# Output projection of an adaLN block as Strassen block products, with all later conditioning sums moved beside the convolution

## The chip, the cores and the metric

The kernel runs as one program on one core of a Trainium2 chip. The metric is the device time of one execution in microseconds (us). TensorE (PE) multiplies, VectorE (DVE) and ScalarE (ACT) work on tiles in on-chip memory, GpSimd (POOL) here mostly issues DMAs that add to what they land on ("accumulate"), and SyncE (SP) issues the plain DMAs. Each engine carries out its instructions in program order; a semaphore wait holds everything behind it on that engine. PEld is the loading of weights into the PE array, which overlaps the matmuls.

## What is computed

One block with 512 tokens and width 2048, all in fp32:

```python
sh_a, sc_a, g_a, sh_f, sc_f, g_f = jnp.split(jax.nn.silu(c) @ ada_w[l] + ada_b[l], 6, axis=-1)
h = modulate(rms_norm(x, norm_mix[l]), sh_a, sc_a)
proj = h @ w_in[l]
...
y_conv = short_conv_mixer(cb, cc, ch, conv_w[l])          # u = cc * ch, 3-tap causal conv, times cb
y_conv = rms_norm(y_conv in groups of 128, out_norm_conv)
y_attn = nsa_mixer(q, k..., v..., gates, ...)             # 8 heads of 128, then rms_norm per head
x = x + g_a[:, None, :] * (jnp.concatenate([y_conv, y_attn], axis=-1) @ w_out[l])
h = modulate(rms_norm(x, norm_ffn[l]), sh_f, sc_f)
x = x + g_f[:, None, :] * ((jax.nn.silu(h @ ffn_w1[l]) * (h @ ffn_w3[l])) @ ffn_w2[l])
```

The six conditioning vectors are 2048 wide each. `w_out` is 2048 x 2048, `ffn_w1` and `ffn_w3` are 2048 x 5632, `ffn_w2` is 5632 x 2048.

## The kernel before

**Products.** An fp32 product is made of three matmuls: both factors are split into a high part that PE takes as it is (`hi`, an ACT cast) and the rest (`lo`, a DVE subtraction), and `mm3` (L96 to L100) adds lo x hi, hi x lo and hi x hi into one bank. A weight tile is 128 x 1024 (`load_split`, L86 to L94): one DMA, one cast, one subtraction.

**Conditioning sums.** A product of silu(c) with a 2048-row, 512-column piece of `ada_w` is not made on PE. It is a chain of 16 DVE operations of 128 x 512 (`ada_steps`, L183 and L185), each of which adds one loaded tile times a column of `cT` into `acc`. The 128 partitions are summed afterwards: four PE transposes (L200) and a DVE reduction (L202) where the result is wanted as a column, or a matmul with ones (`ada_bcast`, L252) where it is wanted as a row. The sums for sh_a and sc_a stand at the start of the kernel. Later come 4 sums for g_a and 8 for sh_f and sc_f; the 4 for g_f run during the up projection, by ACT and POOL (`gate_steps`, L209).

**Stages, with their times in the trace.**

- 0 to 195 us: first sums, norm of x, first columns of `w_in`.
- 195 to 306 us: two `token_blocks` (L612; 16 steps of a weight tile), with the preparation of keys and the compressed blocks woven in.
- 306 to 719 us: `convs` (L807): eight `conv(c)` (L760) of eight steps each, one weight tile 128 x 768 per step, with `attention_steps` woven in. Behind each conv's matmuls stands its tail: product, three taps, gate (L783 to L788), square on ACT (L791), a matmul with ones (L793), rsqrt (L123, L124) and the final multiply (L797). Six of the sums for sh_f and sc_f stand one behind each of conv 0 to 5, the first g_a sum behind conv 7.
- 719 to 915 us: the output projection, `token_block(w_out, ...)` for four column blocks n of 512, 32 weight tiles, 768 matmuls of 128 x 512 into four banks `main`, one for each tile of 128 tokens. After each n: `t = ps * ga` (L868), `x = x + t` (L869), the square with its row sum (L870), a store to the spill `xd` (L871), and for n < 3 the transposes of x into `x2T` (L846, L847). The other three g_a sums and the last two of sh_f and sc_f run here.
- 915 to 928 us: the row norms (L881 to L883), a matmul with ones that spreads them over the partitions (`rb`, L884), the last transposes, then `modulated` (L957 on DVE, L958 on ACT) and the splits of the blocks of the normed input (`h_parts`, L948 and L949) that the up projection multiplies.
- 928 to 1799 us: up projection, Strassen's seven block products for eight in 42 of 44 units (`product`, L932 and L934).
- 1799 to 2241 us: down projection, Strassen's scheme over the token halves, column halves and row pairs: 154 steps of 12 matmuls (L1264), in four groups of 6, 6, 5 and 5 row pairs. Its weight sums are made in place by accumulate DMAs on POOL (L1222), its input sums by DVE (L1230 to L1235).

**What sets the order.** The code is unrolled, and each engine gets its instructions in the order in which the Python code issues them; `weave` mixes two generators by a fixed ratio, and `issue_after` puts an instruction behind another of its engine. There is no planner.

Of the kernel before, what the change touches and what calls it, by code (L numbers as in the profile page):

```python
# [17 lines left out]
P = 128  # L18
# [20 lines left out]
CGL = IN_W - P  # L39

# [29 lines left out]
def block_kernel(ctx: ExitStack, tc: tile.TileContext, a: dict, out: bass.AP):  # L70
# [13 lines left out]

    def load_split(ring, src, ko, n):
# [5 lines left out]
        nc.sync.dma_start(raw[:, :m].rearrange("p (k n) -> p k n", k=ko), src)  # L91
        nc.scalar.copy(hi[:, :m], raw[:, :m])  # L92
        nc.vector.tensor_sub(lo[:, :m], raw[:, :m], hi[:, :m].bitcast(F32))  # L93
        return tuple(t[:, :m].rearrange("p (k n) -> p k n", k=ko) for t in (hi, lo))  # L94
# [32 lines left out]
    accp = pool("acc", 2)  # L127
    act_ = ExitStack()
    act = pool("act", KC, stack=act_)

# [7 lines left out]
    for i in range(NT):  # L138
        xt = sp.tile([P, D], F32, name=f"xt{i}")
        nc.sync.dma_start(xt, x[i * P:(i + 1) * P, :])  # L140
        xts.append(xt)
# [19 lines left out]
    shf = cp.tile([P, 2, KC], F32, name="shf")  # L161
    gfc = cp.tile([P, KC], F32, name="gfc")
# [4 lines left out]
    def ada_steps(ring, width, c0, n, bias=False):  # L167


        acc = accp.tile([P, 512], F32, tag="acc", name="acc")[:, :n]  # L170
# [38 lines left out]
    def gate_steps(ring, lag):  # L209

        for n in range(4):
            acc = accp.tile([P, 512], F32, tag="acc", name="acc")
            c0 = 5 * D + n * 512
            for k in range(KC):
                w = ring.tile([P, 512], F32, tag="araw", name="araw") if k else acc
# [3 lines left out]
                yield  # L219
# [4 lines left out]
                for _ in range(lag - 2):  # L224
                    yield
            gate_cols(acc, n)

    def gate_cols(acc, n):

        ps = main()  # L230
# [3 lines left out]
        d = gfc[:, 4 * n:4 * n + 4]  # L234
        b = bcol[:, 5 * KC + 4 * n:5 * KC + 4 * n + 4]
        v = ps.rearrange("p (c q) -> p c q", c=4)
        if n < 2:
# [6 lines left out]
    latest = {}  # L244

    def note(what):
        latest[what] = nc.cur_bb.bb.instructions[-1]

    def ada_bcast(psum_tile, dst, acc):

        ps = psum_tile()
        nc.tensor.matmul(ps, ones, acc, start=True, stop=True)  # L252
        nc.scalar.copy(dst, ps)
# [6 lines left out]
    kvp = ExitStack()  # L260
    kp = pool("kvraw", 1, stack=kvp, side="right")
    ksv = kp.tile([P, NT, 512], F32, name="ksv")
    q0 = kp.tile([P, NT, 512], F32, name="q0")
# [623 lines left out]
    act_.close()  # L887

# [458 lines left out]
```

## Time and profile before

| | |
|---|---|
| median of 3 runs | 2244.02 us (2242.67 to 2246.96) |
| profiled execution: its time, its span | 2242.84 us, 2241.1 us |
| PE busy, DVE busy, ACT busy, POOL busy (share of the span) | 97%, 78%, 48%, 10% |
| mean granted PE clock | 0.989 |
| DMA, mean over the span | 182 GB/s |

The profiler's span leaves out 1.7 us of the execution's own time. A row of the costliest groups reads: line, engine, operation, output <- inputs, shape, how often | busy time in us, mean ns of one | idle time of the engine just ahead of them and what ended it. A timeline row reads: start, length, engine, line, operation, how many in a row, and in brackets the idle time before and what ended it. Matmuls are pipelined and their ends modelled, so PE's pace is read from the distance of their starts. A row of the windows reads: from:to, length, then the busy time and instruction count of PE, PEld, DVE, ACT and POOL, the granted PE clock, the share of the DMA engines and GB/s.

### The profile page before, as it was taken

The numbers are of one execution on the slowest core, as the hardware profiler recorded it, in microseconds if no ns is written. First come the engines' busy times: TensorE is split into PE (matmuls) and PEld (weight loads), VectorE is DVE, ScalarE is ACT, GpSimd is POOL, SyncE is SP. The second block draws the span as 40 slices with busy tenths as digits, with TensorE's granted clock in tenths as the row PEclk, the third lists the DMA queues.
The fourth block names the chain that finished last, engine by engine and source line by source line (L and its number), as shares of the span: only waits on it lengthen the run. The fifth ranks groups of instructions, "written<-read, shape, count | busy, mean of one in ns | idle before, by whom it ended". The sixth has DMA issues, their size and how long they took to land.

```text
span 2241.1 us, 30371 instructions
## 1 busy us (share of the span) xinstructions
PE 2163.3 (97%) x10999; PEld 1811.5 (81%) x10999; DVE 1745.1 (78%) x2677; ACT 1078.4 (48%) x1790; POOL 226.0 (10%) x265
## 2 busy tenths in 40 slices
PE   5899999999999999899999999999999989999998
PEld 5677778778787778788888888888888868888887
DVE  5886857767866773788888888888888866878787
ACT  6544434555444222645555555555554445545453
POOL 2330000000000000000110110110110021111132
PEclk9999999999999999999999999999999999999999
DMA  8985556345544884266665665666665299998888
GB/s 293 295 270 147 163 180 176 111 116 152 154 134 134 272 310 141 75 188 169 164 179 155 174 169 154 171 170 164 165 174 150 75 278 242 214 229 215 227 167 183
DMA packets 386658, 408.95 MB, mean 182 GB/s; under 512 B 18404, under 2 KB 292168, under 8 KB 385484
## 3 DMA queue, kind: packets, MB, share of 16 engines
q1 hardware_dynamic: 358796, 325.22, 47.2%
q0 software_dynamic: 27712, 81.80, 18.7%
q8 instruction: 86, 1.41, 0.3%
q14 instruction: 64, 0.52, 0.1%
HBM read 371.30 MB, written 19.92 MB: 175 GB/s over the span
## 4 chain that ended last, share of the span: by engine, by line
PE 60%; DMA 3%; DVE 1%; ACT 0%; issue 0%; DVEq 0%; SPq 0%; ACTq 0%
PE main L932 14%; PE aux L932 11%; PE aux L1264 9%; PE main L1264 9%; PE main L934 7%; PE aux L934 6%; PE main L98 1%; PE main L99 1%; PE main L100 1%; DMA g<-gd 1%; DMA araw<-in_ada_w 1%; DMA t<-in_ffn_w 1%; DVE acc L185 0%; DMA raw<-in_ffn_w 0%; DMA acc<-in_ada_b 0%
## 5 line engine op out<-in xcount | busy, mean ns | idle before, releaser
L932 PE MATMUL main<-hC,whi 128*128 128x512 f32 x1408 | 355.5, 394 | 3.5 <-DVE hC L949 3.4
L925 DVE TENSOR_TENSOR wlo<-raw,whi 128x1024 fp32r<-128x1024 f32 x218 | 265.7, 1219 | 106.6 <-ACT whi L919 105.2
L919 ACT CAST whi<-raw 128x1024 fp32r<-128x1024 f32 x218 | 228.6, 1049 | 238.4 <-PE main L932 117.6
L932 PEld LDWEIGHTS main<-hC,whi 128*128 128x128 f32 x1408 | 254.0, 190 | 49.9 <-DVE hC L949 4.3
L932 PE MATMUL aux<-hC,whi 128*128 128x512 f32 x1072 | 270.0, 394 | 0.2 <-ACT whi L919 0.2
L932 PEld LDWEIGHTS aux<-hC,whi 128*128 128x128 f32 x1072 | 193.7, 190 | 35.2 <-ACT whi L919 0.4
L98 PE MATMUL main<-alo,whi 128*128 128x512 f32 x448 | 183.3, 410 | 21.3 <-DVE alo L357 21.0
L934 PEld LDWEIGHTS main<-hC,wlo 128*128 128x128 f32 x1408 | 192.1, 190 | 13.7
L934 PE MATMUL main<-hC,wlo 128*128 128x256 f32 x1408 | 196.3, 282 | 0.0
L185 DVE SCALAR_TENSOR_TENSOR acc<-araw,cT,acc 128x512 f32<-128x512 f32 x184 | 137.7, 749 | 71.0 <-DMA araw<-in_ada_w 67.3
L99 PE MATMUL main<-ahi,wlo 128*128 128x512 f32 x448 | 178.3, 398 | 0.0
L100 PE MATMUL main<-ahi,whi 128*128 128x512 f32 x448 | 177.7, 397 | 0.0
L92 ACT CAST whi<-raw 128x1024 fp32r<-128x1024 f32 (+1 forms) x80 | 78.9, 988 | 191.5 <-PE main L100 123.7
L98 PE MATMUL main<-wlo,ahi 128*128 128x512 f32 x384 | 153.2, 399 | 7.3 <-DVE t L868 7.0
L934 PEld LDWEIGHTS aux<-hC,wlo 128*128 128x128 f32 x1072 | 146.4, 190 | 10.5
L100 PE MATMUL main<-whi,ahi 128*128 128x512 f32 x384 | 151.6, 395 | 0.0
L99 PE MATMUL main<-whi,alo 128*128 128x512 f32 x384 | 151.5, 395 | 0.0
L934 PE MATMUL aux<-hC,wlo 128*128 128x256 f32 x1072 | 149.8, 283 | 0.0
L919 ACT CAST whi<-t 128x1024 fp32r<-128x1024 f32 x84 | 88.3, 1051 | 126.8 <-PE aux L932 63.4
L1216 ACT CAST whi<-t 128x1024 fp32r<-128x1024 f32 x88 | 92.6, 1054 | 111.2 <-PE aux L1264 55.0
L93 DVE TENSOR_TENSOR wlo<-raw,whi 128x1024 fp32r<-128x1024 f32 (+1 forms) x80 | 92.0, 1154 | 67.3 <-ACT whi L92 66.7
L1217 DVE TENSOR_TENSOR wlo<-t,whi 128x1024 fp32r<-128x1024 f32 x88 | 107.4, 1221 | 24.6 <-ACT whi L1216 23.9
(307 smaller groups left out, 4390.5 us busy)
## 6 DMA issues: line engine op xcount, KB each, us to landing
raw<-in_ffn_w SPq DMA_DIRECT2D x220, 512.0 KB, 4.3
araw<-in_ada_w SPq DMA_DIRECT2D x300, 256.0 KB, 3.5
t<-in_ffn_w POOLq DMA_DIRECT2D x66, 512.0 KB, 6.0
raw<-in_w_in SPq DMA_DIRECT2D x128, 192.0 KB, 2.8
raw<-in_w_in SPq DMA_DIRECT2D x40, 512.0 KB, 6.3
araw<-in_ada_w SPq DMA_DIRECT2D x40, 512.0 KB, 5.8
raw<-in_w_out SPq DMA_DIRECT2D x32, 512.0 KB, 3.6
acc<-araw POOLq DMA_DIRECT2D x60, 256.0 KB, 4.2
```

What stands on the lines that cost most here:

```text
L93: nc.vector.tensor_sub(lo[:, :m], raw[:, :m], hi[:, :m].bitcast(F32))
L98: nc.tensor.matmul(ps, lhs[0], rhs[1], start=first, stop=False)
L99: nc.tensor.matmul(ps, lhs[1], rhs[0], start=False, stop=False)
L100: nc.tensor.matmul(ps, lhs[0], rhs[0], start=False, stop=last)
L185: nc.vector.scalar_tensor_tensor(acc, w, s, acc, op0=ALU.mult, op1=ALU.add)
L919: nc.scalar.copy(hi, t)
L925: nc.vector.tensor_sub(lo, t, hi.bitcast(F32))
L932: nc.tensor.matmul(ps, wt[0][:, ks[k]], hC[p][:, k, :], start=first and k == 0, stop=False, skip_group_check=True)
L934: nc.tensor.matmul(ps[:, HS:], wt[1][:, ks[k]], hC[p][:, k, 0:HS], start=False, stop=last and k == HK - 1, skip_group_check=True)
L1216: nc.scalar.copy(hi, w)
L1217: nc.vector.tensor_sub(lo, w, hi.bitcast(F32))
L1264: nc.tensor.matmul(ps, a_[l][:, tok], w[r][:, cs], start=begins and m == 0, stop=ends_ and m == 2, skip_group_check=True)
```

## The change

1. **Output projection by block products.** The four token tiles and 2048 columns are halved, and the 16 row blocks of `w_out` are paired (k with k + 8) in two groups of four pairs. `products()`, which the down projection now uses too, makes seven products p for each group, each of four steps k of 12 matmuls (L965): 56 steps, 672 matmuls. For each step `w_split` casts and subtracts the 128 x 1024 weight tile (L919, L921), `a_split` makes the 128 x 256 input sum and its split (L935 to L947), and POOL adds the next weight block onto the tile in memory (L927). Banks are read by `o_read` into `y2` (L1082 to L1091).
2. **Gate and residual.** The g_a sums are turned to columns `gac` and spread to rows by `gate_rows` (L285: 16 DVE diagonals, 16 matmuls with ones of 128 columns). A finished tile of `y2` is multiplied by `ga` (L1099), and POOL adds x to it from memory (L1100). Then follow its square (L1036, ACT) and its store (L1037, POOL).
3. **Turning by diagonal norms.** `row_norms` makes for each token tile a diagonal matrix of its norms (L1048). 64 matmuls of `y2` with it (L1065) transpose and scale at once; ACT applies gain and shift on the way out (L1069, 128 x 256 each). The upper token half goes first, and three half products of the up projection (L1187, L1189) stand ahead of the lower half. `rb` and L957 are gone.
4. **All 12 later sums earlier.** `sums_stream` puts two DVE sum operations (L241, L243) behind each of the 16 token-block steps and two or three behind each of the 64 conv steps: 32 + 160. Their loads are single tiles, staged in buffers not yet in use.
5. **Conv tails.** The square, ones matmul and norm of conv c (L839 to L844) move behind the first steps of conv c + 1; those of conv 7 stand in the output projection's first group.
6. **Buffers.** Four 128 x 2048 tiles `xy` hold in turn x, the raw keys, the conv and attention outputs, the blocks of the normed input, weight pairs of the up projection and T pairs of the down projection.

```diff
+    def sums_stream():
+        jobs = [(lambda acc, n=n: gate_cols(acc, n, 0, gac), 2 * D + n * 512) for n in range(4)]
...
+                w = spare[0]()
+                with tc.issue_after(latest["load"]):
+                    nc.sync.dma_start(w, ada_v[:, k, c0:c0 + 512])
+                with tc.issue_after(latest["lo"]):
+                    if k:
+                        nc.vector.scalar_tensor_tensor(acc, w, cT[:, k:k + 1], acc, op0=ALU.mult, op1=ALU.add)
...
     def convs():
+            for k in range(KC // 2):
+                next(steps_)
+                if k in (0, 2):
+                    next(last, None)
+                for _ in range(2 + k % 2):
+                    next(stream, None)
+                yield
+            last = steps_
...
+    def x2_store(i, n):
+        y = y2[:, i, n * 512:(n + 1) * 512]
...
+        with tc.issue_after(latest["o_hi"]):
+            nc.scalar.activation(sq, y, AF.Square, accum_out=ss2[:, i, n:n + 1])
+        nc.gpsimd.dma_start(xd[n][:, i, :], y)
...
+    def scaled():
+        i, n = scales.pop(0)
+        cs = slice(n * 512, (n + 1) * 512)
+        nc.vector.tensor_mul(y2[:, i, cs], y2[:, i, cs], ga[:, cs])
+        nc.gpsimd.dma_start(y2[:, i, cs], x[i * P:(i + 1) * P, cs], accum_op=ALU.add)
+        turns.append((i, n))
...
+        if b and p == 4:
+            if k == 0:
+                row_norms(0)
+            scaled()
+            x2_store(*turns.pop(0))
+            if k > 1:
+                modulated(0, 0, 4 * k - 8, aux)
+                split_half(0, 0, 4 * k - 8)
...
-        for i, ps in enumerate(pst):
-            nc.vector.tensor_mul(t, ps, ga)
-            nc.vector.tensor_add(x2, x2, t)
-            nc.scalar.activation(t, x2, AF.Square, accum_out=ss2[:, i, n:n + 1])
-        nc.gpsimd.dma_start(xd[n], x2s[n])
...
+    products(w_out, o_groups, ((1, 5, 6, 3, 7, 2, 4), (1, 5, 6, 3, 2, 7, 4)), 1,
...
+    for c in (0, 4):
+        modulated(0, 1, c, aux)
+        split_half(0, 1, c)
...
+    while turns:
+        x2_store(*turns.pop(0))
+    row_norms(1)
...
+    for s in order[:3]:
+        s["mm"](s, (0,))
+    for j in range(2):
+        for c in (0, 4):
+            modulated(1, j, c, (aux, main)[c // 4])
+            split_half(1, j, c)
```

**DVE in the convolution, before:** the weight splits (`wlo`, L772) among attention (L714 to L740) and the sums (L185, `acc <- araw`) that wait their turn behind a conv.

```order
L772 TENSOR_TENSOR wlo<-raw,whi 128x768
L715 TENSOR_REDUCE nm<-aux 128x1
L781 MEMSET u 128x2
L185 SCALAR_TENSOR_TENSOR acc<-araw,cT,acc 128x512
L772 TENSOR_TENSOR wlo<-raw,whi 128x768
L720 RECIPROCAL sm<-sm 128x2
L185 SCALAR_TENSOR_TENSOR acc<-araw,cT,acc 128x512
L721 TENSOR_TENSOR sm<-sm,gts 128x2
```

The same engine in the convolution after the change, where `xy` is the staging buffer and L820 the split:

```order
L241 SCALAR_TENSOR_TENSOR acc_3568<-xy,cT,acc_3568 128x512
L761 TENSOR_REDUCE nm<-aux 128x1
L241 SCALAR_TENSOR_TENSOR acc_3568<-xy,cT,acc_3568 128x512
L820 TENSOR_TENSOR wlo<-raw,whi 128x768
L766 RECIPROCAL sm<-sm 128x2
L241 SCALAR_TENSOR_TENSOR acc_3568<-xy,cT,acc_3568 128x512
L767 TENSOR_TENSOR sm<-sm,gts 128x2
L786 SCALAR_TENSOR_TENSOR o_3438<-aux,sm,o_3438 128x128
L243 TENSOR_SCALAR acc_3944<-xy,cT 128x512
```

The sums now stand in every step between two splits, in all eight convs.

**ACT from the output projection to the up projection, before** (`whi` of L919 is a weight of the up projection, L958 the shift, L948 a split of the normed input):

```order
L870 ACTIVATE t,ss_6478<-x_7214 128x512 x2
L919 CAST whi<-raw 128x1024
L870 ACTIVATE t,ss_6478<-x_7214 128x512 x2
L123 ACTIVATE r_7807<-r_7807,eps_t 128x1
L123 ACTIVATE r_7814<-r_7814,eps_t 128x1
L123 ACTIVATE r_7821<-r_7821,eps_t 128x1
L123 ACTIVATE r_7828<-r_7828,eps_t 128x1
L958 ACTIVATE x2T<-x2T,shf 128x512
```

And after; here L919 casts the last `w_out` weights, L946 is a split of a projection input, L1174 a weight of the up projection:

```order
L919 CAST whi<-t 128x1024
L1036 ACTIVATE t,ss_6541<-y_6540 128x512 x2
L946 CAST phi<-xy 128x256
L919 CAST whi<-t 128x1024
L1036 ACTIVATE t,ss_6541<-y_6540 128x512 x2
L919 CAST whi<-t 128x1024
L1036 ACTIVATE t,ss_6541<-y_6540 128x512
L919 CAST whi<-t 128x1024
L133 ACTIVATE rs_6542<-rs_6542,eps_t 128x2
L1174 CAST whi<-raw 128x1024
L1036 ACTIVATE t,ss_6541<-y_6540 128x512 x2
L1174 CAST whi<-raw 128x1024
```

The squares stood behind the last weight casts; now they stand between the casts of the projection's last steps and of the first up products.

**POOL at the same place, before:** one store of a whole column block, with the residual added on DVE.

```order
L174 MEMSET acc 128x512 x2
L871 DMA xd_6415<-x_6481 128x2048
L871 DMA xd_6416<-x_6848 128x2048
L871 DMA xd_6417<-x_7214 128x2048
L984 DMA gd_6418<-d_8129 128x512
```

After, for the last tiles, the adding of x (L1100) and the stores (L1037):

```order
L1100 DMA y_6540<-in_x 128x512
L1037 DMA xd_6463<-y_6540 128x512
L1100 DMA y_6540<-in_x 128x512 x2
L1037 DMA xd_6464<-y_6540 128x512
L1100 DMA y_6540<-in_x 128x512
L1037 DMA xd_6463<-y_6540 128x512
L1037 DMA xd_6464<-y_6540 128x512
L1100 DMA y_6540<-in_x 128x512 x2
L1037 DMA xd_6465<-y_6540 128x512
L1100 DMA y_6540<-in_x 128x512
```

Additions and stores alternate in one queue; each store waits for the landing of the addition onto its tile.

More of the change, by code (lines that the diff above doesn't have):

```diff
@@ L1 @@
+import itertools
 from contextlib import ExitStack
@@ L39 @@
 CGL = IN_W - P
+SIGN = (1, 1, -1, -1)
 PI2_A = 6.28125
@@ L126, in block_kernel, with big @@
     ring = rings(ctx, 4, 3)
-    accp = pool("acc", 2)
+    accp = pool("acc", 1)
+    xy = pool("xy", 4)
     act_ = ExitStack()
     act = pool("act", KC, stack=act_)
+    def big():
+        return xy.tile([P, D], F32, tag="xy", name="xy")
     st0 = ExitStack()
@@ L223, in gate_steps, with gate_cols @@
                     nc.gpsimd.dma_start(acc, w, accum_op=ALU.add)
-                for _ in range(lag - 2):
+                for _ in range(lag - lag // 2):
                     yield
-            gate_cols(acc, n)
-    def gate_cols(acc, n):
-        ps = main()
+            gate_cols(acc, n, 1, gfc)
+    def gate_cols(acc, n, which, to):
+        ps = (aux, main)[which]()
         for c in range(4):
@@ L242, in gate_cols, with gate_rows @@
             nc.vector.tensor_sub(d, d, b)
[L244 to L253, printed above, removed]
+    def gate_rows(row, col, tile_of, temp):
+        for n in range(4):
+            ps = tile_of()
+            for c in range(4):
+                dg = temp.tile([P, P], F32, tag="dg", name="dg", bufs=2)
+                nc.vector.tensor_scalar(dg, ident, col[:, 4 * n + c:4 * n + c + 1], None, op0=ALU.mult)
+                nc.tensor.matmul(ps[:, c * P:(c + 1) * P], ones, dg, start=True, stop=True)
+            nc.scalar.copy(row[:, n * 512:(n + 1) * 512], ps)
     pp = pool("ps", 4, space=PSUM)
@@ L877, in block_kernel @@
-    rb = aux()
-    for i in range(NT):
-        dg = tp.tile([P, P], F32, tag="dg", name="dg")
-        r2 = tp.tile([P, 1], F32, tag="r2", name="r2")
-        nc.vector.reduce_sum(r2, ss2[:, i, :], axis=AX)
-        rsqrt(r2, r2, D)
-        nc.vector.tensor_scalar(dg, ident, r2, None, op0=ALU.mult)
-        nc.tensor.matmul(rb[:, i * P:(i + 1) * P], ones, dg, start=True, stop=True)
-    x2_turned(3)
+    HS, HK = S // 2, KC // 2
+    half = [slice(0, HS), slice(HS, S)]
+    BLOCK = {1: (0, 0), 2: (0, 0), 5: (1, 1), 7: (1, 1), 6: (0, 1), 3: (0, 1), 4: (1, 0)}
@@ new lines, in h_parts, with modulated @@
+    def h_parts(p, src, k0, n):
+        hi, lo = hC[p][:, k0:k0 + n, 0:HS], hC[p][:, k0:k0 + n, HS:S]
+        nc.scalar.copy(hi, src)
+        nc.vector.tensor_sub(lo, src, hi.bitcast(F32))
+    def modulated(i, j, c, bank):
+        if (i, j) not in A:
+            A[i, j] = big().rearrange("p (k t) -> p k t", k=HK)
+        for k in (c, c + 2):
+            ps = bank()
+            with tc.issue_after(latest["mm"]):
+                for e in range(4):
+                    f = (j * HK + k + e // 2) * P
+                    nc.tensor.matmul(ps[:, e * P:(e + 1) * P], y2[:, 2 * i + e % 2, f:f + P], dgs[i, e % 2],
+                                     start=True, stop=True)
+            for e in range(2):
+                f = j * HK + k + e
+                nc.scalar.activation(A[i, j][:, k + e, :], ps[:, half[e]], AF.Identity, scale=gsc[:, 1, f:f + 1],
+                                     bias=shf[:, 1, f:f + 1])
```

569 lines of the change are left out of this document (315 added, 254 removed).

## The prediction

> **What bounds the kernel now.** I read the page first, then the stages around the change in the windows, then PE's timeline where the windows show it idle.
>
> ```profile
> span 2241.1 us, 30371 instructions
> PE 2163.3 (97%) x10999; PEld 1811.5 (81%) x10999; DVE 1745.1 (78%) x2677; ACT 1078.4 (48%) x1790; POOL 226.0 (10%) x265
> ```
>
> PE sets the time. The change can gain in two ways: by fewer matmuls, and by filling the holes in PE. The windows show that the holes lie around the output projection:
>
> ```profile
> 680.00:735.00 55.00, 50.60 (x210) 39.76 (x208) 37.51 (x45) 22.29 (x32) 0.52 (x1) 0.94 0.37 116
> 775.00:820.00 45.00, 40.40 (x182) 32.95 (x181) 32.59 (x43) 10.44 (x14) 1.28 (x2) 0.98 0.84 286
> 915.00:928.00 13.00, 5.27 (x27) 4.39 (x25) 11.31 (x27) 8.98 (x21) 0.53 (x1) 0.85 0.42 129
> ```
>
> PE's timeline says what ends each hole, and gives PE's pace:
>
> ```profile
> 687.50 2.08 PE L793 MATMUL aux<-cc,const 128*128 128x512 f32 x2 [4.40 <-ACT cc L791]
> ...
> 819.04 0.79 PE L98 MATMUL main<-wlo,ahi 128*128 128x512 f32 x1 [4.60 <-DVE t L868]
> ...
> 911.73 0.39 PE L98 MATMUL main<-wlo,ahi 128*128 128x512 f32 x1
> ...
> 914.91 0.39 PE L100 MATMUL main<-whi,ahi 128*128 128x512 f32 x1
> 919.10 0.68 PE L884 MATMUL aux<-dg,const 128*128 128x128 f32 x4 [3.80 <-DVE dg L883]
> ...
> 927.88 2.08 PE L932 MATMUL main<-hC,whi 128*128 128x512 f32 x4 [3.19 <-DVE hC L949]
> ...
> 934.89 1.09 PE L932 MATMUL main<-hC,whi 128*128 128x512 f32 x4
> ```
>
> From 911.73 to 914.91 there are 14 starts, so a 128x512 matmul costs 0.227 us. The first hole is a conv's tail (L791 feeds L793), the second the wait for the banks to be read (L868), the third the row norms and the making of the normed input. A hole costs more than its length, because the granted clock (the number before the DMA share) falls to half behind it:
>
> ```profile
> 686.00:690.00 4.00, 2.50 (x5) 1.35 (x6) 2.85 (x4) 2.25 (x4) 0.00 (x0) 0.50 0.36 98
> 690.00:692.00 2.00, 2.00 (x8) 1.62 (x7) 1.66 (x1) 0.31 (x1) 0.52 (x1) 0.52 0.72 198
> 818.00:824.00 6.00, 4.96 (x16) 3.88 (x17) 5.99 (x11) 2.38 (x5) 0.53 (x1) 0.52 0.98 345
> 1822.00:1824.00 2.00, 1.73 (x4) 1.44 (x5) 2.00 (x5) 0.79 (x1) 0.86 (x1) 0.50 1.07 276
> ```
>
> Behind the hole at 683 the clock is 0.5 for some 4.4 us (half of which, 2.2 us, is lost); behind the one at 815 for about 5 us and then lower for a while (some 2.9 us lost).
>
> **The change part by part.** The rows for the output projection are grouped here by form, from 718 to 928 us, and after them those of the down projection, whose scheme and shapes the new output projection takes over:
>
> ```profile
> L98 PE MATMUL main<-wlo,ahi 128*128 128x512 f32 x256 | 102.1, 399 | 7.0 <-DVE t L868 7.0
> L870 ACT ACTIVATE t<-x 128x512 f32<-128x512 f32 x16 | 10.0, 628 | 32.5 <-DVE x L869 32.5
> L846 PE MATMUL aux<-const,x 128*128 128x128 f32 x64 | 10.4, 314 | 0.0
> L252 PE MATMUL aux<-acc,const 128*128 128x512 f32 x8 | 4.3, 618 | 0.0
> L884 PE MATMUL aux<-dg,const 128*128 128x128 f32 x8 | 2.0, 353 | 4.5 <-DVE dg L883 4.5
> L200 PE MATMUL aux<-const,acc 128*128 128x128 f32 x8 | 1.7, 354 | 0.0
> ...
> ```
>
> ```profile
> L1264 PE MATMUL main<-wlo,phi 128*128 128x512 f32 x308 | 121.0, 393 | 4.2 <-DVE wlo L1217 4.2
> L1217 DVE TENSOR_TENSOR wlo<-t,whi 128x1024 fp32r<-128x1024 f32 x88 | 107.4, 1221 | 24.6 <-ACT whi L1216 23.9
> L1216 ACT CAST whi<-t 128x1024 fp32r<-128x1024 f32 x88 | 92.6, 1054 | 111.2 <-PE aux L1264 55.0 <-PE main L1264 53.8 <-DMA t<-in_ffn_w 1.5
> L1242 DVE TENSOR_TENSOR plo<-g,phi 128x256 fp32r<-128x256 f32 x88 | 36.7, 418 | 2.3 <-ACT phi L1241 2.2
> L1241 ACT CAST phi<-g 128x256 fp32r<-128x256 f32 x88 | 35.3, 402 | 0.0
> L1289 DVE TENSOR_TENSOR y<-aux,y 128x512 f32<-128x512 f32 x44 | 30.1, 685 | 4.9 <-PE aux L1264 4.8
> L1284 POOL DMA_DIRECT2D y<-xd x12 | 10.3, 878 | 29.6 <-DVE y L1283 29.6
> L1298 PE MATMUL aux<-dg,const 128*128 128x128 f32 x32 | 5.9, 301 | 1.2 <-DVE dg L1297 1.1
> ```
>
> *Matmuls.* 768 become 672: 96 x 0.227 = 21.8 us less. The small ones cancel: the 8 of L252 (4.3 us) and 8 of L884 (2.0) go, 16 of the kind of L1298 (16 x 0.18 = 3.0) come for the gate rows, 16 more of the kind of L200 (16 x 0.21 = 3.4) turn the g_a sums to columns, and the 64 transposes of L846 become 64 diagonal matmuls of the same size. Term: -21.8.
>
> *Holes that go.* The tail of conv 6 gets other matmuls in front of it: 4.4 + 2.2 = 6.6 us. The waits for L868 (7.0 us in all, the row of L98) go with their slow clock: 7.0 + 2.9 = 9.9, because two sets of four banks now alternate. From 915.14, the end of the projection (0.227 behind the last start), to 934.89, where up runs at full pace, are 19.75 us. In them lie 8 matmuls of L884, 16 of L846 and 16 of L932, which at full pace are 24 x 0.07 (my estimate: a quarter of 0.227 and a little) + 16 x 0.227 = 5.3; so 14.4 us are lost. Together 30.9 us of hole. Term: -30.9, if nothing takes their place; the next three terms are what does.
>
> *Holes that come, at the start and within.* The first T tiles of `w_out` and the first input splits stand behind the last conv's work: four sums, 14 small splits (14 x 0.42 = 5.9 us of DVE) and the first 1.22 us of `wlo` against 12 us of conv matmuls that are still queued. I take 1.5 us, between 0 and 4. Within the stage, DVE has 56 x (1.22 + 0.42) = 91.8 for the splits, 32 x 0.42 = 13.4 for the input sums, 44 x 0.685 = 30.1 for the reads, 16 x 0.685 = 11.0 for the gate, and some 4.6 for the gate diagonals: 151 us beside 672 x 0.227 = 152.5 us of PE plus some 8 for the small matmuls. That is 94% of PE's time. Where the down projection runs the same steps with less DVE work, its 154 steps lose 4.2 us on one set of banks. A product that continues on the banks just read (3 to 2 on one set, 7 to 4 on the other) must wait for DVE. I take 5 us, between 0 and 14.
>
> *The hand-over to the up projection.* This is the largest unknown. The price of a POOL addition is the row of L1284, 0.88 us to issue, and its landing:
>
> ```profile
> raw<-in_ffn_w POOLq DMA_DIRECT2D x22, 512.0 KB, 8.5
> ...
> y<-xd POOLq DMA_DIRECT2D x16, 256.0 KB, 5.1
> ```
>
> In the last eight steps (products 7 and 4 of the second group, 21.8 us of PE) POOL has eight additions of x and their stores in one queue, and a store waits until its tile's addition has landed. So the queue moves by about 5.1 + 0.6 us at each such wait: counted from the start of product 7, the four tiles of product 2 land at about 8, 13, 14 and 19 us, those of product 7 at 25 to 32. Their squares (L870's kind, 0.63 and 0.19 for reading the sum) stand in ACT's queue ahead of the last casts of `w_out`. The third cast of product 4 comes behind the square of the tile that lands at 14, the last behind the one of 19; then the reduction, rsqrt, the reciprocal, the last `wlo` (1.22) and two diagonals bring PE its next work near 23.5 where it could take it at 20. Behind that, ACT stands on the four squares of product 7 until about 33, although PE only waits for the upper half's evacuations (16 of 0.40 and four casts of 1.05 for a half). I get the first up matmul at 37, its second half at 39.5, the lower half's at 53 to 56, and an unbroken stream from 61. From the end of product 7 (10.9) to there are 50 us, and the work in them is 10.9 (product 4) + about 8 (diagonal matmuls) + 14.5 (the up matmuls) = 33. So 17 us are lost, 20 with the slow clock behind a hole of 9. Term: +20. With landings as quick as 2 us and the squares out of the way it is 10; with landings of 8.5 us (the upper row) it is 30.
>
> The Trainium skill's page "DMA: Bandwidth & Descriptors", section "Anatomy of one DMA — SWDGE (gpsimd) path", fits a GpSimd DMA by 2.0 us + bytes / 436e3, an estimate of 2.6 us for 256 KB. By it the sum would be some 8 us lower. The row has 5.1 for an addition, and the measurement decides.
>
> *The sums beside the conv.* Here DVE is given more:
>
> ```profile
> 195.00:250.00 55.00, 54.80 (x248) 44.23 (x247) 42.58 (x103) 30.39 (x77) 0.62 (x2) 1.00 0.45 128
> 250.00:306.00 56.00, 55.37 (x306) 39.07 (x305) 30.96 (x73) 15.75 (x37) 0.00 (x0) 1.00 0.61 194
> 306.00:718.00 412.00, 405.05 (x2024) 326.54 (x2024) 302.93 (x622) 198.83 (x445) 1.05 (x2) 0.99 0.49 141
> ...
> 231.00:243.00 12.00, 11.80 (x55) 9.41 (x54) 11.93 (x39) 7.84 (x25) 0.31 (x1) 1.00 0.55 165
> ```
>
> ```profile
> L185 DVE SCALAR_TENSOR_TENSOR acc<-araw,cT,acc 128x512 f32<-128x512 f32 x106 | 79.3, 748 | 50.4 <-DMA araw<-in_ada_w 49.7
> L772 DVE TENSOR_TENSOR wlo<-raw,whi 128x768 fp32r<-128x768 f32 x64 | 61.0, 953 | 10.2 <-ACT whi L771 9.7 <-issue 0.2
> ```
>
> Before, the 306 to 718 us have 106 + 6 sum operations, after 160: 48 x 0.75 = 36 us more in 412, so DVE goes from 74% (302.93) to 82%. A conv step lasts 412 / 64 = 6.4 us; DVE's work in it grows from 4.7 to 5.3. It fits on average; a queue of sums ahead of a `wlo` can still make PE wait now and then. In the token blocks, 32 operations (24 us) come into 111 us with 37.5 us of idle DVE time, of which two thirds lie in the second half; at 231 DVE is full. The new loads also stand in SP's queue ahead of the weights of later steps, which are two to three steps early. I take 4 us for both stages, between 0 and 20. All of the added work uncovered would be 60.
>
> *The rest.* The down projection computes what it did, with T in pairs; the up projection's loads move, with the same matmuls. I set 0, within 3 either way.
>
> **Sum.** -21.8 - 30.9 + 1.5 + 5 + 20 + 4 = -22.2. From the profiled execution's 2242.84 us this gives 2220.6; the median of the runs lies 1.2 us above that execution, so 2222 us. A difference of less than 0.2% (4.5 us) can't be told from none.
>
> **The rivals.**
>
> 1. *The hand-over and the nearly full DVE eat half of it* (2234 us). If landings go with 8.5 us (+10), or DVE's 94% costs 14 in place of 5 (+9), about 12 us more are lost. For it: both queues are in order, and three engines wait for one another there. Against: the down projection's steps lose only 4.2 us.
> 2. *The hand-over is covered* (2206 us). If the additions land within 2 us, the squares never stand in the way, ten go from the term of 20; with 3 less in each of the two terms for the projection and the conv it is 16 less. For it: DMA is at 0.42 there. Against: the 5.1 us row.
> 3. *Slower: DVE becomes the bound beside the conv* (2253 us). The mechanism is the sum operation that stands ahead of a `wlo` in DVE's order. It decides once 26 of the added 60 us, in place of my 4, find no idle DVE time in their own step: then the 22 us of gain are gone. With 35 uncovered the time is 2222 + 31 = 2253. For it: DVE at 11.93 of 12 in the token blocks, and attention that comes in bursts. Against: 26% of idle time in the conv, of which 49.7 us were waits of sums for their own loads, which spread loads do not repeat.
> 4. *The clock stays at half through the whole hand-over* (2234 us). The row 1822 to 1824 shows 0.50 behind a hole of only 2.8 us:
>
> ```profile
> 1822.27 0.80 PE L1264 MATMUL main<-wlo,phi 128*128 128x512 f32 x1 [2.80 <-DVE wlo L1217]
> ```
>
> The hand-over has several holes of 2 to 9 us with short work between. If the clock were at half for 30 of its 50 us, the 24 us of work that I have at full pace would take 12 more than my 3. The page "TensorE: Matmul & The Clock Gate" of the Trainium skill, section "What's actually happening", has the clock fall after an idle window of about 3.4 us and return after as long a busy one. By that rule the 2.8 us hole would not do it unless the window begins earlier; the row shows that it does, so shorter holes count. With only the hole of 9 us slowing the clock, the forecast stands; with none, it is 3 us less.
> 5. *No change* within 0.2%: the up projection's loads, now tied to the release of the `xy` tiles, come late by as much as is gained. Nothing in the profile speaks for so much.
>
> **How the numbers follow.** The forecast (2212 to 2230) has 0.52, rivals 1 and 4 together 0.20, rival 2 0.12, rival 3 0.10, rival 5 0.06. Faster by over 0.2% is below 2239.5: 0.52 + 0.12 + nearly all of 0.20 = 0.83. Slower by over 0.2% is above 2248.5: most of rival 3 and a little of 5, 0.09. The rest, 0.08, is the same. The range holds the forecast, rival 2, and rivals 1 and 4 with some margin for the conv's term: 2204 to 2241.
>
> **What would show it.** In the new profile: 672 matmuls of L965, in a stage of 155 to 170 us; no wait of a conv's ones matmul above 1 us; PE busy above 97% between 306 and 718; in the hand-over POOL stores (L1037) waiting about 5 us for L1100, ACT's squares (L1036) waiting for L1100, and holes of 15 to 20 us in all ahead of L1187. I am wrong if PE waits for `wlo` L820 by more than 10 us, if the hand-over loses less than 12 or more than 30, or if the up or down projection changes by more than 3 us.

## The result, and the profile after

The changed kernel takes 2221.97 us (median of 4 runs, 2218.94 to 2223.04), the kernel before 2243.35 us beside it (4 runs, 2241.85 to 2246.96). The ratio is 0.990, with a 95% interval of 0.9883 to 0.9917: faster by 1.0%. The forecast was 2222 us.

The page of the changed kernel:

```profile
span 2221.3 us, 30757 instructions
PE 2150.8 (97%) x10999; PEld 1805.2 (81%) x10999; DVE 1797.8 (81%) x2795; ACT 1110.0 (50%) x1863; POOL 273.5 (12%) x321
```

PE has 12.5 us less work, and the span is 19.8 us shorter. Three marks in PE's timelines divide this: the first matmul of the output projection, its last, and the first of the down projection.

| stretch | before | after | difference |
|---|---|---|---|
| start to the first matmul of the output projection | 718.70 | 714.78 | -3.9 |
| from there to its last one's end | 196.4 | 175.8 | -20.6 |
| from there to the first of the down projection | 892.2 | 897.0 | +4.8 |
| from there to the end | 433.8 | 433.7 | -0.1 |

The projection pays, the convolution pays, and the hand-over to the up projection costs some of it. The convolution pays more than the first row says: from the ones matmul of conv 0 to that of conv 6 it takes 307.0 us in place of 313.6. The rest of the first stretch is 2.7 us longer, and it varies by 3.8 us between profiles of kernels with the same code there. The split between the last two rows is not firm either. In a second profile of the changed kernel they are 894.3 and 437.2 us; counted to the last matmul of the up projection instead, the two profiles have 6.6 and 6.9 us more than before behind the projection's end.

These windows answer to those of before (from:to, length, then PE, PEld, DVE, ACT, POOL, clock, DMA share, GB/s):

```profile
306.00:718.00 412.00, 411.41 (x2077) 333.21 (x2076) 336.28 (x685) 193.33 (x439) 2.16 (x3) 1.00 0.59 177
...
873.40:878.00 4.60, 4.49 (x10) 3.09 (x11) 2.90 (x4) 0.72 (x2) 1.83 (x3) 0.50 0.84 132
...
898.00:905.50 7.50, 5.48 (x24) 5.19 (x25) 5.29 (x7) 6.98 (x14) 2.71 (x5) 0.50 0.51 186
```

Beside the convolution DVE went from 302.93 to 336.28 us (+33, forecast +36), and PE is busy for 411.41 of 412. The holes stand later. PE's timeline from 714 us to the first full up products has all but seven of them here. Of the other seven, four are waits for `wlo` (L921) in the first steps of the projection, 3.9 us together, and three are waits of the gate rows (L292) for DVE's diagonals, 1.7 us:

```profile
873.41 0.79 PE L965 MATMUL main<-wlo,phi 128*128 128x512 f32 x1 [3.80 <-DVE y L1086]
...
885.98 2.05 PE L1065 MATMUL aux<-dn,y 128*128 128x128 f32 x16 [0.90 <-DVE dn L1048]
...
893.37 1.16 PE L1065 MATMUL aux<-dn,y 128*128 128x128 f32 x8 [0.80 <-ACT xy L1069]
898.06 2.08 PE L1065 MATMUL aux<-dn,y 128*128 128x128 f32 x8 [3.53 <-ACT xy L1069]
902.09 3.79 PE L1065 MATMUL aux<-dn,y 128*128 128x128 f32 x16 [1.96 <-ACT xy L1069]
```

The waits between 862 and 875 us show who stands behind the first (engine, output and line, whom it waited for: us, how often, longest). It must be read upwards: PE waits for a bank to be read, DVE could not read it because it stood on an input split, the split waited for ACT, and ACT stood on the square of a tile whose addition had not landed. POOL waited for the same landing, to store the tile.

```profile
POOL xd L1037 <- DMA y<-in_x: 8.7, 3, 5.4
ACT t L1036 <- DMA y<-in_x: 5.4, 1, 5.4
DVE plo L947 <- ACT phi L946: 4.9, 1, 4.9
...
PE main L965 <- DVE y L1086: 3.8, 1, 3.8
```

This is POOL's queue there, an addition (L1100) and a store (L1037) in turn:

```profile
865.15 0.94 POOL L1100 DMA_DIRECT2D y<-in_x  x1
871.48 0.56 POOL L1037 DMA_DIRECT2D xd<-y  x1 [5.40 <-DMA y<-in_x]
872.02 1.83 POOL L1100 DMA_DIRECT2D y<-in_x  x2
876.63 0.58 POOL L1037 DMA_DIRECT2D xd<-y  x1 [2.77 <-DMA y<-in_x]
```

### The profile page after: what moved, and what is told of

Its sections match the earlier page's. It is cut to its first block, busy times and chain, and to the rows that moved or that the text cites. A ratio compares the mean times of both kernels' runs of the same rounds, so it can differ in the third digit from the quotient of the medians.

```text
span 2221.3 us, 30757 instructions
## 1 busy us (share of the span) xinstructions
PE 2150.8 (97%) x10999; PEld 1805.2 (81%) x10999; DVE 1797.8 (81%) x2795; ACT 1110.0 (50%) x1863; POOL 273.5 (12%) x321
## 4 chain that ended last, share of the span: by engine, by line
PE 82%; DVE 6%; DMA 6%; issue 3%; ACT 1%; POOL 1%; SPq 0%; DVEq 0%; POOLq 0%; ACTq 0%
PE main L1187 15%; PE aux L1187 11%; PE main L965 10%; PE aux L965 10%; PE main L1189 8%; PE aux L1189 6%; PE main L108 5%; PE main L110 5%; PE main L109 5%; PE aux L783 2%; DMA t<-in_w_out 1%; PE aux L755 1%; DMA y<-in_x 1%; DVE acc L326 1%; DMA raw<-in_w_in 1%
## 5 line engine op out<-in xcount | busy, mean ns | idle before, releaser
L1187 PE MATMUL main<-hC,whi 128*128 128x512 f32 x1408 | 355.1, 394 | 0.0
L1187 PEld LDWEIGHTS main<-hC,whi 128*128 128x128 f32 x1408 | 253.6, 189 | 46.0 <-DVE hC L1054 0.5
L1187 PE MATMUL aux<-hC,whi 128*128 128x512 f32 x1072 | 268.6, 392 | 0.0
L1187 PEld LDWEIGHTS aux<-hC,whi 128*128 128x128 f32 x1072 | 192.6, 189 | 34.0
L1180 DVE TENSOR_TENSOR wlo<-xy,whi 128x1024 fp32r<-128x1024 f32 x135 | 164.5, 1219 | 64.3 <-ACT whi L1174 64.2
L1174 ACT CAST whi<-xy 128x1024 fp32r<-128x1024 f32 x135 | 141.5, 1048 | 146.8 <-PE main L1187 76.8
L1189 PEld LDWEIGHTS main<-hC,wlo 128*128 128x128 f32 x1408 | 192.2, 190 | 14.3
L1189 PE MATMUL main<-hC,wlo 128*128 128x256 f32 x1408 | 196.2, 282 | 0.0
L965 PE MATMUL main<-wlo,phi 128*128 128x512 f32 x420 | 167.1, 399 | 12.3 <-ACT phi L946 4.5
L965 PE MATMUL main<-whi,phi 128*128 128x512 f32 x420 | 166.0, 395 | 0.0
L965 PE MATMUL main<-whi,plo 128*128 128x512 f32 x420 | 166.0, 395 | 0.0
L965 PE MATMUL aux<-wlo,phi 128*128 128x512 f32 x420 | 164.3, 391 | 0.0
L965 PE MATMUL aux<-whi,plo 128*128 128x512 f32 x420 | 163.6, 390 | 0.0
L965 PE MATMUL aux<-whi,phi 128*128 128x512 f32 x420 | 163.5, 389 | 0.0
L1189 PEld LDWEIGHTS aux<-hC,wlo 128*128 128x128 f32 x1072 | 146.2, 190 | 10.5
L919 ACT CAST whi<-raw 128x1024 fp32r<-128x1024 f32 x90 | 94.9, 1055 | 114.7 <-PE aux L965 60.0
L1174 ACT CAST whi<-t 128x1024 fp32r<-128x1024 f32 x84 | 88.2, 1049 | 123.1 <-PE aux L1187 63.2
L919 ACT CAST whi<-xy 128x1024 fp32r<-128x1024 f32 x88 | 92.9, 1055 | 113.4 <-PE main L965 55.4
L1189 PE MATMUL aux<-hC,wlo 128*128 128x256 f32 x1072 | 149.5, 282 | 0.0
```

What stands on the lines that cost most here:

```text
L919: nc.scalar.copy(hi, wt)
L965: nc.tensor.matmul(ps, at_k[l][:, tok], wt[r][:, cs], start=begins and m == 0, stop=ends_ and m == 2, skip_group_check=True)
L1174: nc.scalar.copy(hi, t)
L1180: nc.vector.tensor_sub(lo, t, hi.bitcast(F32))
L1187: nc.tensor.matmul(ps, wt[0][:, ks[k]], hC[p][:, k, :], start=first and k == 0, stop=False, skip_group_check=True)
L1189: nc.tensor.matmul(ps[:, HS:], wt[1][:, ks[k]], hC[p][:, k, 0:HS], start=False, stop=last and k == HK - 1, skip_group_check=True)
```

## The experiments

The kernels were run in three lists, each on one chip. Times are medians of four to twelve runs, beside the kernel before on the same chip. The kernel before took 2243.4 to 2247.0 us on these chips, so kernels from different lists are compared by their ratios to the kernel before. On the chip of the second list the changed kernel was run again.

> The changed kernel itself again, so that the runs of this list can be compared with it on one chip: 22 us faster than before, within 2 us.

Measured: 2223.09 us, ratio 0.9909 (0.9893 to 0.9924).

**Do the sums cost anything beside the convolution?** All but the first of the 16 terms of each later sum are left out:

```diff
-                    if k:
-                        nc.vector.scalar_tensor_tensor(acc, w, cT[:, k:k + 1], acc, op0=ALU.mult, op1=ALU.add)
-                    else:
+                if not k:
+                    w = spare[0]()
...
```

> Leaves out 15 of the 16 operations and loads of each of the 12 later sums (180 DVE operations, 180 loads), so the conditioning vectors are wrong. Theory A (the added DVE work finds idle DVE time beside the token blocks and the conv, and costs PE nothing): the time stays within 2 us of the changed kernel, 2220 to 2223. Theory B (sums ahead of a weight split make PE wait): 4 us or more faster, 2218 or less. In the trace, the stretch to the first L965 matmul (714.8 us) shrinks by under 1.5 us by A, by 4 or more by B.

> The run without 180 of the 192 later sum operations and their loads again, on a chip on which the kernel with late squares and stores runs too, since the first such run had no changed kernel beside it. Theory A (the sums cost PE nothing): the stretch from the ones matmul of conv 0 to that of conv 6 lasts 306 to 307 us as in the changed kernel (385.70 to 692.68), and the time is within 2 us of the changed kernel's (about 0.990 of before). Theory B: that stretch is 3 us or more shorter and the time 4 us or more lower.

Measured: 2218.47 us at 0.9873 (0.9858 to 0.9888) in the first list, 2218.48 us at 0.9888 (0.9864 to 0.9911) in the third. By the ratios this is 3 to 8 us under the changed kernel, between the two theories, and the times can't decide. The traces do for the convolution. From the ones matmul of conv 0 to that of conv 6 it takes 306.1 us, against 307.0 and 306.7 in the two profiles of the changed kernel. This is the window of the repeat, beside the changed kernel's 411.41 and 336.28 above:

```profile
306.00:718.00 412.00, 411.81 (x2081) 334.09 (x2081) 240.85 (x534) 194.76 (x440) 2.78 (x3) 1.00 0.30 81
```

95 us of DVE work gone, 0.4 us of PE time won. The sums cost PE under 1 us in the convolution, as theory A says. They are not free everywhere: the projection takes 173.3 and 172.8 us in the two runs without them, against 175.8 and 175.3 in the two profiles of the changed kernel, and 1 to 2 us of that are shorter waits for `wlo` in its first steps. The rest of the difference is not settled. The stretch up to the first matmul of the projection alone took between 711.3 and 715.2 us in the profiles of kernels that differ only behind it.

**Why are they free?** The tails of conv 0 to 6 go back to where they were before, right behind their conv:

```diff
                 yield
-            last = steps_
-        rest.append(last)
+            if c < 7:
+                for _ in steps_:
+                    pass
+            last = iter(()) if c < 7 else steps_
+        rest.append(last)
```

> The tail of each conv but the last (taps, square, ones matmul, norm) is put back right behind that conv's steps, as before the change; all else as in the changed kernel. Theory A (the delayed tails removed the hole of 4.4 us and its slow clock at the end of conv 6): a hole of 3 to 5 us comes back at the end of conv 6, 4 to 7 us slower than the changed kernel. Theory B (the hole came from the sums that stood behind conv 6 in DVE's order, and is gone with them): no hole above 1.5 us, within 1.5 us of the changed kernel.

Measured: 2239.38 us at 0.9978 (0.9969 to 0.9988), 16.3 us slower than the changed kernel on that chip. Neither theory had this. The hole of 3 to 5 us at the end of conv 6 did not come back (1.8 us there); instead PE waits at the ends of several convs, and the stretch from conv 0's ones matmul to conv 6's takes 323.5 us in place of 306.7. Here are three of the largest waits of PE up to the up projection, and the window:

```profile
PE main L109 <- DVE wlo L820: 6.3, 5, 1.8
...
PE aux L841 <- ACT raw L839: 3.0, 1, 3.0
...
PE aux L783 <- ACT pr L765: 2.2, 2, 1.7
```

```profile
306.00:718.00 412.00, 399.65 (x2000) 321.38 (x2001) 321.57 (x657) 188.42 (x429) 0.00 (x0) 0.99 0.54 164
```

DVE's timeline at the end of a conv shows why: the tail's first multiplication waits for the conv's last matmul, and the next conv's `wlo`, which PE needs at once, is queued behind it.

```profile
423.43 0.69 DVE L831 TENSOR_TENSOR raw<-main,raw 128x512 f32<-128x512 f32 x1 [2.01 <-PE main L110]
424.16 0.49 DVE L833 TENSOR_SCALAR xy<-raw,cols 128x512 f32<-128x512 f32 x1
424.68 0.75 DVE L834 SCALAR_TENSOR_TENSOR xy<-raw,cols,xy 128x511 f32<-128x511 f32 x1
425.47 0.75 DVE L835 SCALAR_TENSOR_TENSOR xy<-raw,cols,xy 128x510 f32<-128x510 f32 x1
426.13 0.95 DVE L820 TENSOR_TENSOR wlo<-raw,whi 128x768 fp32r<-128x768 f32 x1
```

PE waits 1.78 us for that `wlo` at 427.14. So in this kernel the late tails are needed for the sums to be free, and without them the outcome comes close to my third rival (DVE as the bound beside the conv): nearly all of the gain is gone. That the two hold each other up is shown in part only. The kernel before has its tails in place and 48 fewer sum operations beside the convs, and its stretch takes 313.6 us, 9.9 less than here; but its tails also have tiles of their own, where those of the changed kernel use a weight buffer (`raw`, L830). No run has the tails in place without the sums, or with their own tiles.

**What were the waits for L868 in the kernel before?** The five sums in its output projection are left out (the first gate column block serves for all):

```diff
-        if n < 3:
-            acc_g = ada(aring, 1024, 2 * D + (n + 1) * 512, 512, bias=True)
-        turn_cols = ffn_cols(aring, 1024, 6 + n) if n < 2 else None
+        turn_cols = (lambda j=6 + n: ada_cols(aux, acc_g, 1, 1 - j % 2, j // 2 * 4, 4)) if n < 2 else None
```

> The kernel before, with the five sums left out that stand in its output projection (80 DVE operations and 40 loads); the gate of the first column block is used for all, and two pieces of shift and scale are wrong. Theory A (my prediction's: the banks cause the waits for L868, since four banks must be read before the next column block can begin): 5 us or more of the 7.0 us of waits remain, at most 3 us faster than before. Theory B (the sums in DVE's queue delay the reads): under 1.5 us of the waits remain and the slow clock goes too, 8 to 11 us faster than before.

Measured: 2229.23 us, ratio 0.9939 (0.9925 to 0.9953), 14 us faster than before. The waits for L868 are gone from PE's list; in the projection PE is busy without a hole, and it takes 185.8 us where it took 196.4:

```profile
720.00:906.00 186.00, 186.00 (x836) 151.51 (x835) 65.25 (x75) 52.98 (x79) 1.82 (x3) 1.00 0.36 121
```

This is theory B, with 10.6 us in that stage: one set of four banks is enough once the sums are gone. The other 3 to 4 us lie outside the stage and are within what profiles differ by. DVE's timeline of the kernel before shows the same. PE stood from 814.4 to 819.0 us for a bank, and its read (L868) stood behind sums, one of which waited for its own load, and a weight split:

```profile
815.05 1.54 DVE L185 SCALAR_TENSOR_TENSOR acc<-araw,cT,acc 128x512 f32<-128x512 f32 x2 [1.13 <-DMA araw<-in_ada_w]
816.51 1.22 DVE L93 TENSOR_TENSOR wlo<-raw,whi 128x1024 fp32r<-128x1024 f32 x1
817.64 0.75 DVE L185 SCALAR_TENSOR_TENSOR acc<-araw,cT,acc 128x512 f32<-128x512 f32 x1
818.30 0.68 DVE L868 TENSOR_TENSOR t<-main,ga 128x512 f32<-128x512 f32 x1
```

Whether a second set of banks would also have removed the waits, with the sums left in place, no run shows.

This run also says what the block products are worth. From the first matmul of the projection to the last of the up projection it takes 1080.9 us before, 1069.6 here, and 1066.8 and 1066.6 in the two profiles of the changed kernel. So 11 us of the gain come with the sums gone from that stage alone; block products and new hand-over together add only about 3.

**What makes the hand-over dear?** Squares, evacuations and stores are moved, apart and together. First the squares: those of product 2's last tiles and of product 7's tiles go behind the casts of the last weights.

```diff
         if b and p == 7:
...
             scaled()
-            for _ in range((1, 2, 2, 3)[k]):
+            for _ in range((0, 1, 1, 1)[k]):
                 x2_store(*turns.pop(0))
         if b and p == 4:
-            if k == 0:
+            for _ in range((2, 3, 0, 0)[k]):
+                x2_store(*turns.pop(0))
+            if k == 1:
                 row_norms(0)
...
```

> Same computation. The squares of the last tiles stand two to five ACT instructions later, behind the casts of the projection's last weights, and the stores of the tiles stand behind all additions in POOL's queue. Theory A (POOL's stores that wait for landings, and ACT's squares that wait for them ahead of casts, make the holes at 873 and 898): the hole of 3.8 us at the start of product 4 goes with 2.4 us of slow clock, the holes ahead of the up matmuls shrink by 3 to 5 us: 8 to 11 us faster than the changed kernel, 2211 to 2214. Theory B (the hand-over is bound by how much ACT has to do there): the work only moves, 0 to 4 us faster.

Measured: 2214.38 us at 0.9858 (0.9842 to 0.9875), 9 to 11 us faster than the changed kernel by the ratios. The code issues the stores late too, but in POOL's queue they still stand between the additions:

```profile
861.29 0.92 POOL L1107 DMA_DIRECT2D y<-in_x  x1
867.44 0.56 POOL L1044 DMA_DIRECT2D xd<-y  x1 [5.22 <-DMA y<-in_x]
867.98 1.83 POOL L1107 DMA_DIRECT2D y<-in_x  x2
```

So a queue does not always have the order of the code, although the part on the kernel says so: between code and queue the stores were moved forward. This run therefore tests the squares and not the stores. The hole at 873 is gone, and one larger hole stands ahead of the diagonals:

```profile
881.09 1.22 PE L1072 MATMUL aux<-dn,y 128*128 128x128 f32 x4 [6.69 <-DVE dn L1055]
```

In the next one DVE also takes every second evacuation of the turned tiles (the gain and shift as `tensor_scalar` with two column operands).

> Same computation, as the one before in this list, and half of the 32 evacuations of the turned tiles go to DVE. ACT's work in the hand-over falls by 16 x 0.45 = 7.2 us, DVE's rises by as much. If after the reordering ACT is what is late (theory B of the one before, or what is next by theory A): 3 to 5 us faster again. If POOL's landings or the chain of norms are late: within 1.5 us of the one before.

Measured: 2216.01 us at 0.9863 (0.9848 to 0.9878): no gain. The hole of 6.7 us ahead of the diagonals stays as it was, and it waits for DVE's `dn`, the diagonals of the norms. So the norms were late, not ACT's amount of work.

Then, with the squares late as in the first of these, the stores are held behind the last addition (`issue_after`), and the first diagonals behind the projection's last step:

```diff
+            with tc.issue_after(latest["add"]):
+                nc.gpsimd.dma_start(xd[n][:, i, :], y2[:, i, n * 512:(n + 1) * 512])
...
-            if k > 1:
-                modulated(0, 0, 4 * k - 8, aux)
-                split_half(0, 0, 4 * k - 8)
+            if k == 3:
+                for c in (0, 4):
+                    modulated(0, 0, c, aux)
+                    split_half(0, 0, c)
```

> Same computation. As the run with late squares, and now POOL's stores are also held behind all twelve additions, and the first diagonal matmuls stand behind the projection's last 12 matmuls instead of ahead of them. Theory A (the additions' landings set the upper half's norms): the last of the upper tiles lands 1 to 4 us earlier, the hole of 6.7 us ahead of the diagonal matmuls shrinks by that and by the 2.7 us of matmuls that now fill it: 4 to 6 us faster than the run with late squares, about 12 to 15 faster than the changed kernel. Theory B (DVE's reads and gate multiplications, one per step, set the landings, not the stores): the hole shrinks by 2.7 us alone, 2 to 3 us faster than the run with late squares.

> The kernel with late squares, stores behind all additions and diagonal matmuls behind the projection's last 12 matmuls again: 0.983 to 0.985 of the time before, 15 to 18 us under the changed kernel.

Measured: 2206.21 us at 0.9835 (0.9819 to 0.9852), and again 2206.33 us at 0.9828 (0.9811 to 0.9845). This is the fastest version, with the same computation: 16.9 us under the changed kernel on the same chip. PE goes from the projection to the diagonals without a hole:

```profile
878.20 7.31 PE L1073 MATMUL aux<-dn,y 128*128 128x128 f32 x64
885.27 1.18 PE L1203 MATMUL main<-hC,whi 128*128 128x512 f32 x4
```

Last, the stores alone, with the same `issue_after` and ACT's queue as in the changed kernel:

> The changed kernel with nothing moved but POOL's stores of the finished tiles, which stand behind all additions; ACT's order is the same. Theory A (stores that wait for landings hold up the additions behind them, and that makes most of the hand-over's loss): landings come up to 5 us earlier, the holes at 893 to 902 shrink by half or more, 6 to 10 us faster than the changed kernel. Theory B (the squares' place in ACT's order makes most of it): the hole of 3.8 us at 873 stays and the others shrink by less than 2 us, under 3 us faster.

Measured: 2209.34 us at 0.9842 (0.9825 to 0.9859), 13 to 15 us under the changed kernel by the ratios. That is more than theory A expected. The hole at 873 is gone although the squares stand where they stood, because the additions are no longer held up. In the changed kernel the gate multiplications of four tiles begin at 858.5, 861.1, 863.8 and 866.4 us, and their additions at 865.2, 872.0, 872.6 and 877.2. Here each addition follows its gate multiplication by 1.0 us. This is POOL's queue, for the same additions, each waiting only for its gate multiplication (L1107):

```profile
857.32 0.86 POOL L1108 DMA_DIRECT2D y<-in_x  x1 [3.52 <-DVE y L1107]
859.99 0.86 POOL L1108 DMA_DIRECT2D y<-in_x  x1 [1.81 <-DVE y L1107]
862.66 0.86 POOL L1108 DMA_DIRECT2D y<-in_x  x1 [1.81 <-DVE y L1107]
865.28 0.86 POOL L1108 DMA_DIRECT2D y<-in_x  x1 [1.77 <-DVE y L1107]
```

And the waits in the hand-over, of the changed kernel from 862 to 906 us:

```profile
POOL xd L1037 <- DMA y<-in_x: 24.6, 10, 5.4
ACT t L1036 <- DMA y<-in_x: 20.6, 8, 5.4
```

and of this one from 850 to 892 us:

```profile
ACT t L1036 <- DMA y<-in_x: 6.7, 4, 2.4
...
POOL xd L1045 <- DMA y<-in_x: 2.4, 2, 1.4
```

The additions took no less time to land, 6.6 us in the median in both kernels between 800 and 910 us, so it is their place in the queue that made the difference. The stores were the root, and the squares passed the delay on. Moving either removes the hole at 873.

**The diagonal products.** PE's rows have 128 records for the 64 diagonal matmuls; 64 transposes had 64. Both stand 0.112 us apart:

```profile
774.76 1.96 PE L846 MATMUL aux<-const,x 128*128 128x128 f32 x16
776.56 1.12 PE L252 MATMUL aux<-acc,const 128*128 128x512 f32 x2
```

```profile
914.70 1.95 PE L1065 MATMUL aux<-dn,y 128*128 128x128 f32 x16
916.48 1.95 PE L1065 MATMUL main<-dn,y 128*128 128x128 f32 x16
```

The first row is of before (16 transposes in 1.80 us), the second of the changed kernel (8 diagonals in 1.78). To see what the second record is worth, all but eight are made plain transposes, in the changed kernel and in the fastest one; the norm is left out of most of the normed input:

```diff
+                    if j == 0 and k == 0:
...
+                    else:
+                        nc.tensor.transpose(ps[:, e * P:(e + 1) * P], y2[:, 2 * i + e % 2, f:f + P], ident)
```

> All turning matmuls but the first four of each token half are plain transposes with the identity, so the norm is left out of most of the normed input. The trace of the changed kernel has 128 records for the 64 diagonal matmuls, the one before 64 for 64 transposes, both 0.112 us apart. Theory A (each fp32 product by a diagonal takes PE two passes, and I mis-sized it): 56 x 0.112 = 6.3 us of PE work go; half of it stands where PE waits for ACT anyway, so 3 to 6 us faster. Theory B (the hand-over is bound by ACT's evacuations and casts throughout): less than 1.5 us faster.

> The same kernel with all but eight of its 64 diagonal matmuls as plain transposes, so the norm is left out of most of the normed input. In the changed kernel this edit gained nothing that could be told. Theory A (there PE waited for ACT; here PE is what is late in the hand-over, and 56 x 0.112 us of second passes go): 4 to 6.5 us faster than the kernel beside it. Theory B (ACT's evacuations and squares are just behind PE and become late): under 2.5 us faster.

Measured: 2221.44 us at 0.9889 (0.9874 to 0.9904) for the changed kernel, 2207.84 us at 0.9833 (0.9815 to 0.9850) for the fastest one, where 2206.33 stood beside it. For the fastest one that is no gain. For the changed kernel the ratio is 2 to 5 us lower, within the intervals, and the traces decide: from the first matmul of the projection to the last of the up projection it takes 1067.2 us against 1066.8 and 1066.6. So theory B holds both times. The 6.3 us of PE work turn largely into waits. In the fastest kernel PE's holes behind the projection grow from 2.3 us to 7.0, most of it for the splits that ACT and DVE make from the evacuated tiles:

```profile
903.75 0.50 PE L1206 MATMUL main<-hC,whi 128*128 128x512 f32 x1 [3.58 <-DVE hC L1062]
```

The second record of the diagonals costs PE time but not kernel time. That fits a hand-over in which ACT takes about as long as PE even in the fastest version; no run lightens ACT's work in that version.

## Why the prediction was right, and where its steps were not

The time, 2221.97 us, is within 0.1 us of the forecast. That closeness is luck: the terms are not as good, some errors cancelled, and the changed kernel's own runs lie 4 us apart. The terms against the profile:

| term | forecast | measured | from |
|---|---|---|---|
| 96 matmuls fewer | -21.8 | -21.8 | 672 records of L965, same pace |
| small matmuls | 0 | +9.5 | -2.2 (L252) -0.9 (L884) +3.6 (32 records of L292) +1.8 (16 transposes) +7.2 (diagonals) |
| holes that go | -30.9 | -29.9 | with transposes at 0.112 the old hand-over held 6.3 us of work, not 5.3 |
| start, within, hand-over | +26.5 | +23.3 | 16.6 us of holes and 6.7 of slow clock between 714 and 921 |
| sums beside the conv | +4 | under 1 | the runs without sums, in the conv |

The slow clock is worked out from the windows: half of 4.49 and of 5.48 us of work at 0.50, and some 1.7 in the windows 878 to 880 (0.57), 894 to 898 (0.85) and 905.5 to 908 us (0.69). The measured terms add up to -18 to -19; the profiles differ by 19.8.

- **Matmul count: right.** But that the gain of the change nearly equals it is chance. By the table the block products, the new small matmuls and the new hand-over against the old (13.4 us of loss, in the third row) come to -21.8 + 9.5 + 23.3 - 13.4 = -2.4 us; the other 16.5 us are the holes of the convolution and of L868, which the move of sums and tails removed. The runs agree: 3 us with the hand-over as it is. With POOL's stores moved the stretch takes 1053.2 us in place of 1069.6, so that the block products pay 16.
- **Small matmuls: mis-sized by 9.5 us**, the largest error. I set the 64 diagonal products equal to the 64 transposes "of the same size". A row I had quoted spoke against it: L884 has 8 records for the 4 products of its loop, L846 has 64 for 64. In these traces an fp32 product that is not a transpose is recorded twice. It cost the time little, since it lies where PE waits for ACT: with plain transposes the kernel is no faster.
- **The L868 holes: right in size, wrong in cause.** The prediction said they go "because two sets of four banks now alternate". The kernel before without the five sums has none of them, with its one set of banks. So the move of the sums was enough to remove them; the wait was for a read that stood behind sums in DVE's queue, which the prediction had not followed.
- **The conv hole: right in size (6.6 us from conv 0 to conv 6, as forecast), but the late tails and the sums were costed as if apart.** With the tails back and the sums in every step, the 82% that I worked out for DVE on average did not help, because one in-order queue put a `wlo` behind a wait for PE. That is the outcome of rival 3, with a tail in front of the `wlo` where I had named a sum. How much of it is the tails' doing without the sums stays open.
- **The hand-over: right in mechanism and near in size:** 11.0 us of holes and 6.7 of slow clock, 17.7 in place of 20. Two of the signs that I gave missed: the holes ahead of L1187 were to be 15 to 20 us, and the stage 155 to 170 us, where it took 175.8. The queue on POOL, the squares in front of casts and the evacuations on ACT came as described. My trace by hand put the first large hole ahead of the diagonals; it stood at the start of product 4 (873 us), where a square held up an input split, which I had not followed. An addition took longer than the 5.1 us I used: 6.6 in the median between 800 and 910 us. The estimate of 2.6 us, by the fit on the Trainium skill's page "DMA: Bandwidth & Descriptors", section "Anatomy of one DMA — SWDGE (gpsimd) path", is further off than the row; the measurement decides.
- **Rival 2 (the hand-over covered, 2206 us) is what the kernel gives with POOL's stores moved**: 2206 to 2209. It was forecast for quick landings; it came with slow landings and a better order.
- **Rival 4 (half clock throughout) did not come**, though the clock was at 0.50 behind the holes of 3.80 and 3.53 us. That agrees with the idle window of about 3.4 us on the Trainium skill's page "TensorE: Matmul & The Clock Gate", section "What's actually happening"; the hole of 2.80 us in the kernel before, with 0.50 behind it, does not.

## What to carry to other kernels

When a step goes to a DMA that adds in place, look at what stands behind it in the issuing engine's queue: one store that waits for a landing delays every later addition, and each engine that uses the landed tiles inherits the delay. Work added to an engine with idle time was free here only while nothing in that engine's queue waited for the engine it feeds ahead of that engine's next input; move such waits behind the urgent work first. Measure each part of a change without the others: here the moved sums paid at once, and the block products mostly after the stores were moved. And check the order in the queue, not in the code, before an experiment is read.

## What the hardware showed unexpectedly

In these traces a 128-column fp32 product by a diagonal takes PE 0.22 us, a transpose of a tile of the same size 0.11. The landings of GpSimd's DMAs in the changed kernel between 800 and 910 us:

```profile
t<-in_w_out POOLq DMA_DIRECT2D x12, 512.0 KB, 8.1
y<-in_x POOLq DMA_DIRECT2D x16, 256.0 KB, 6.6
xd<-y POOLq DMA_DIRECT2D x16, 256.0 KB, 3.4
```

A 256 KB addition from GpSimd took 6.6 us to land in the hand-over, where the prediction's row had 5.1 in the down projection, a 512 KB one 8.1, and a plain store of 256 KB 3.4.
